# A macaron layer on one core: in the second FFN, chunk 1 takes plain products for two quarters and seven products for the other two

## The chip, the core and the metric

The kernel runs on one core of a Trainium2 chip. The metric is device time in microseconds. Three runs of the kernel before are shown, and one further execution was profiled; every time of a single instruction below comes from that profiled execution and counts from the start of its span.

## What is computed

One streaming-encoder layer on 1,024 prompt frames and 32 sample frames, 1,024 channels, all in float32. It is a half-step SwiGLU FFN, a mixer (a convolution branch and a recurrent branch), a second half-step SwiGLU FFN, and a last norm. The part that matters here is the second FFN:

```python
def _swiglu_half_step(x, g_pre, g_post, w_in, w_out):
    h = _rmsnorm(x, g_pre)
    gate, up = jnp.split(h @ w_in, 2, axis=-1)
    return x + 0.5 * _rmsnorm((jax.nn.silu(gate) * up) @ w_out, g_post)

x = x + _rmsnorm(merged @ w_out[l], g_mix_post[l])
x = _swiglu_half_step(x, g_ffn2_pre[l], g_ffn2_post[l], w_ffn2_in[l], w_ffn2_out[l])
x = _rmsnorm(x, g_final[l])
```

`w_in` has 1,024 rows and 2 x 2,816 columns. In the steps below, the norm ahead of the mixer's residual is `d`, and the norm that makes `h` for the second FFN is `e`.

## The kernel before, in words

**Layout.** Channels lie on the 128 partitions, and the 1,056 frames are cut into four quarters of 264 (`q` = 0 to 3). Quarters 0 and 1 form pair 0, quarters 2 and 3 form pair 1. The FFN's inner width is cut into 22 chunks of 128 (`i` = 0 to 21). Each float32 operand is split into a high and a low part (`split`: ScalarE copies the high part, line 93; VectorE subtracts to get the low part, line 90), and every product is three matmuls: high times high, high times low, low times high (`mm3`, lines 204 to 206).

**Two ways to make a chunk.** The plain way (`plain`, with `gemm`) makes gate (`pg`) and up (`pu`) of one quarter by 8 x 3 matmuls each, so 48 matmuls for a quarter. It needs that quarter's normed parts and the weight blocks `wh_i`, `wl_i`. The other way (`swiglu`, with `w_ops`) makes gate and up of a pair of quarters with seven products in place of eight, each over half of the channels: 7 x 4 x 3 = 84 matmuls for a pair. It needs sums of the pair's parts (`x_sums`: tiles `t`, and more `xh`, `xl`) and sums of the weights (`w_ops`: tiles `s`, `w`), both made on VectorE and ScalarE.

**The start of the second FFN.** The residual and norm chain of quarter 2 starts (`finish_w`) before the last 48 matmuls of the mixer's output product `pwo`, that of quarter 3 after them. Each chain is: three small matmuls add up squares over the partitions (`pst_d`, line 230), VectorE scales (`r_d`), GpSimd raises to the power -0.5 (`q_d`, line 234), three small matmuls spread the result over the lanes (`pst_d`, line 240), VectorE multiplies `ym` by it and adds the residual `xr_d`, ScalarE squares (`sq_e`), VectorE adds the squares (`ss_e`); then the same for norm `e` (`pst_e`, `r_e`, `q_e`, `pst_e`); then VectorE scales the channels (`f_e`, line 270) and `split` makes the parts `xh`, `xl` (`xhp`, `xlp` for the first half of the channels of an odd quarter), one half of the channels after the other.

**What sets the order.** Each engine runs its own list from the front to the end, and a scheduler makes the lists from the program's order and from priorities. The small matmuls of a chain don't stand where the chain is written: `after(n, f)` puts them off until `n` further products have been issued (12 ahead of the squares' sum of `d`, 6 ahead of the spreading, 30 ahead of the squares' sum of `e`), so they stand between other matmuls. Where the next quarter is wanted sooner than that, `drain()` issues all that was put off at once, for every quarter that waits:

```python
            if q not in h:
                drain()
            for i in range(np):
                plain(i, q)
```

Before, the second FFN makes chunks 0 and 1 in the plain way for all four quarters (`np` = 2), quarter by quarter, and then chunks 2 to 21 by seven products. The first FFN already has the form that the change gives to the second one.

Of the kernel before, what the change touches and what calls it, by code (L numbers as in the profile page):

```python
# [41 lines left out]

TAIL1, TAIL2, TAILW, OG = 4, 3, 2, 2

NP = (3, 2)

BG = (8, 3, 3, 8, 10, 9)

# [6 lines left out]
def macaron_kernel(ctx: ExitStack, tc: tile.TileContext, a: dict, o: dict):  # L55
# [27 lines left out]
    def TMP(name):  # L83
        return tp.tile([P, N], F32, tag="t", name=name)
# [4 lines left out]
    def tt(out, x, y, op):  # L89
        return nc.vector.tensor_tensor(out, x, y, op=op)  # L90
# [91 lines left out]
    def block(src, name, ahead=AHEAD, lead=0):  # L182
        with tc.high_priority(offset=ahead):
            with tc.high_priority(offset=lead):
                w = raw_block(src, name)
            h, l = (ring.tile([P, D], F32R, tag="r", name=f"w{x}_{name}") for x in "hl")
            newest_split[:] = split(h, l, w)
        return h, l
# [27 lines left out]
    def gemm(blk, h, q, name):  # L216
        b = BANK(name)[:, :N]
        while q not in h:
            later.pop(0)[1]()
        for k in range(KC):  # L220
            hi, lo = h[q][k // HC]
            mm(b, blk, k, hi[:, k % HC, :], lo[:, k % HC, :], k == 0, k == KC - 1)
        return b
# [132 lines left out]
    def x_sums(r, fe, fo, name):  # L356
        t = QUAD(F32, f"t_{name}")

        def op(k, v):
            r[k] = (QUAD(F32R, f"xh{k}_{name}"), QUAD(F32R, f"xl{k}_{name}"))  # L360
            split(*r[k], v)

        tt(t, fo[0], fe[0], OP.subtract)
        op("5", t)
        tt(t, fo[1], t, OP.subtract)
        op("6", t)
        tt(fo[0], fo[1], fo[0], OP.subtract)
        op("7", fo[0])
        tt(t, fe[1], t, OP.subtract)
        op("4", t)  # L370
# [93 lines left out]
    def ffn(x, f, h, first, mid, w_in, w_out, early, between, finish, tail, n):  # L464
# [11 lines left out]
        def in_block(i, j):  # L476
            blks.append(block(w_in[2 * i + j], f"i{n}_{i}_{j}", AHEAD if n == 2 else 0, 0 if n == 2 else 2000 if i or j else 4000))
# [5 lines left out]
        q0 = list(newest_part) if n == 1 else []  # L483
        np = NP[n - 1]
        for i in range(np):
# [6 lines left out]
        def plain(i, q):  # L492
            pg = gemm(blks[2 * i], h, q, f"pg{n}_{i}_{q}")
            pu = gemm(blks[2 * i + 1], h, q, f"pu{n}_{i}_{q}")

            def gate(pg=pg, pu=pu):
                t = TMP(f"si{n}_{i}_{q}")
                if q in held:
                    u = TMP(f"su{n}_{i}_{q}")
                    tt(t, rows[q], pg, OP.mult)  # L500
                    tt(u, rows[q], pu, OP.mult)
                    pg, pu = t, u
                nc.scalar.activation(t, pg, AF.Silu)
                tt(t, t, pu, OP.mult)
                nc.sync.dma_start(hd[i, :, q * N:(q + 1) * N], t)

            if q in held and q not in rows:
                held[q].append(gate)
            else:
                gate()  # L510

        for q in range(NQ):
# [9 lines left out]
            if c is not None:  # L522
                while builds:
                    builds.pop(0)()
                x_sums(x[c], f[2 * c], f[2 * c + 1], f"{n}_{c}")
        both = np
        if n == 1:

            both = np + 1
            for j in range(2):  # L530
                in_block(np, j)
            for q in (2, 3):
                plain(np, q)
        for i in range(np, NF):
            with behind_parts(q0 if i == np else []):
                w = w_ops(w_in[2 * i], w_in[2 * i + 1], f"{n}_{i}", WAHEAD if i < both + 2 else WLATE)
# [7 lines left out]
        for c in range(2):  # L544
# [32 lines left out]
            both = {}  # L577
# [95 lines left out]
    def finish1(q, y, ss):  # L673
# [3 lines left out]
        post1(q, y, ss, lambda: rstd(sumsq(y, f"c{q}"), f"c{q}", parts_of, CHAIN))  # L677

    finish1_last = ffn(X1, f1, {}, first1, small_constants, a["w_ffn1_in"], a["w_ffn1_out"], early1, lambda: again(0), finish1, TAIL1, 1)


# [297 lines left out]
    def finish2(q, y, ss):  # L979
# [13 lines left out]
        post_norm(y, q, ss, x2, None, f"g{q}", then)  # L993

    ffn(X2, f2, h2, lambda q, h: None, lambda: None, a["w_ffn2_in"], a["w_ffn2_out"], finish2, lambda: None, finish2, TAIL2, 2)()
    drain()

# [51 lines left out]
```

## Time and profile before

| what | value |
|---|---|
| median of three runs | 2357.35 us (2356.26 to 2358.23) |
| the profiled execution, its own time | 2356.62 us |
| its span | 2354.0 us |
| PE busy | 2323.5 us, 99% of the span, 19,148 matmuls |
| DVE (VectorE) busy | 1467.3 us, 62% |
| ACT (ScalarE) busy | 988.6 us, 42% |
| POOL (GpSimd) busy | 39.9 us, 2% |

Matmul records overlap, so a matmul's cost is the distance from its start to the next start, not its duration. Where a row ends in square brackets, the engine stood idle before it, for so long and until the named instruction was done.

### The profile page before, as it was taken

How to read it: one execution, taken by the hardware profiler on the slowest of the kernel's cores; microseconds unless marked ns; L12 is line 12 of the kernel's file. 1: busy time of each engine (PE TensorE's matmuls, PEld its weight loads, DVE VectorE, ACT ScalarE, POOL GpSimd, SP SyncE). 2: the span in 40 equal slices, each digit the busy share in tenths (PEclk: the TensorE clock that was granted, in tenths of full speed). 3: DMA queues.
4: the chain of work that ended last, by engine and by line, in shares of the span. 5: the costliest groups of instructions: out<-in, count | busy, mean ns of one | idle time of the engine just before them, and what ended most of it. 6: DMA issues, size and time to landing. Idle time of an engine off the chain costs nothing.

```text
span 2354.0 us, 44900 instructions
## 1 busy us (share of the span) xinstructions
PE 2323.5 (99%) x19148; PEld 2317.8 (98%) x19148; DVE 1467.3 (62%) x2289; ACT 988.6 (42%) x1708; POOL 39.9 (2%) x63
## 2 busy tenths in 40 slices
PE   8999999999999999999999999999999999999996
PEld 8999999999999999999999999999999999999996
DVE  6955544542657887897778966459754444542646
ACT  5533333432444554345553444244433333442432
POOL 0000000000000000000000000001000000000000
PEclk9999999999999999999999999999999999999998
DMA  5222222353655222222222554444222222353553
GB/s 177 85 82 82 78 77 74 127 192 100 237 163 179 67 92 74 83 73 83 72 76 74 184 193 166 149 133 149 80 78 77 74 82 78 123 185 106 169 175 129
DMA packets 126521, 275.17 MB, mean 117 GB/s; under 512 B 16753, under 2 KB 58737, under 8 KB 126321
## 3 DMA queue, kind: packets, MB, share of 16 engines
q1 hardware_dynamic: 126320, 272.31, 34.5%
q8 instruction: 149, 2.44, 0.4%
q14 instruction: 52, 0.42, 0.1%
HBM read 213.59 MB, written 58.67 MB: 116 GB/s over the span
## 4 chain that ended last, share of the span: by engine, by line
PE 93%; DVE 3%; DMA 1%; issue 1%; ACT 1%; POOL 0%; SPq 0%; POOLq 0%; DVEq 0%
PE p L204 11%; PE p L206 11%; PE p L205 11%; PE po L205 7%; PE po L204 7%; PE po L206 7%; PE pm L204 3%; PE pm L206 3%; PE pm L205 3%; PE pcv L204 1%; PE pco L204 1%; PE pcg L204 1%; PE pro L204 1%; PE prx L204 1%; PE prg L204 1%; PE prg L206 1%
## 5 line engine op out<-in xcount | busy, mean ns | idle before, releaser
L206 PE MATMUL p<-xh,w 128*128 128x264 f32 x2156 | 609.4, 284 | 0.2 <-DVE w L90 0.2
L205 PE MATMUL p<-xl,w 128*128 128x264 f32 x2156 | 609.4, 283 | 0.0
L204 PE MATMUL p<-xh,w 128*128 128x264 f32 x2156 | 607.1, 284 | 1.5 <-DVE prod L90 0.8
L205 PEld LDWEIGHTS p<-xl,w 128*128 128x128 f32 x2156 | 405.6, 188 | 0.0
L206 PEld LDWEIGHTS p<-xh,w 128*128 128x128 f32 x2156 | 404.9, 188 | 0.4 <-DVE w L90 0.4
L204 PEld LDWEIGHTS p<-xh,w 128*128 128x128 f32 x2156 | 402.6, 188 | 2.6 <-ACT p L93 1.3
L205 PE MATMUL po<-hl,wh_o 128*128 128x264 f32 x1408 | 397.9, 285 | 0.6 <-DVE hl L90 0.6
L206 PE MATMUL po<-hh,wl_o 128*128 128x264 f32 x1408 | 396.6, 284 | 0.0
L204 PE MATMUL po<-hh,wh_o 128*128 128x264 f32 x1408 | 392.1, 286 | 0.4 <-ACT hh L93 0.3
L205 PEld LDWEIGHTS po<-hl,wh_o 128*128 128x128 f32 x1408 | 264.8, 188 | 1.3 <-DVE hl L90 1.3
L206 PEld LDWEIGHTS po<-hh,wl_o 128*128 128x128 f32 x1408 | 264.4, 188 | 0.0
L204 PEld LDWEIGHTS po<-hh,wh_o 128*128 128x128 f32 x1408 | 260.8, 188 | 1.1 <-ACT hh L93 1.0
L90 DVE TENSOR_TENSOR wl_o<-w_o,wh_o 128x1024 fp32r<-128x1024 f32 x109 | 132.9, 1222 | 116.5 <-ACT wh_o L93 116.2
L90 DVE TENSOR_TENSOR p<-p,s 128x264 f32<-128x264 f32 x77 | 33.7, 440 | 267.3 <-ACT p L93 267.3
L721 DVE SCALAR_TENSOR_TENSOR pq<-u,vec,pq 128x542 f32<-128x542 f32 (+14 forms) x232 | 170.8, 768 | 0.0
L93 ACT ACTIVATE wh_o<-w_o 128x1024 fp32r<-128x1024 f32 x109 | 115.3, 1063 | 121.4 <-PE po L205 114.1
L90 DVE TENSOR_TENSOR w<-s,w 128x512 fp32r<-128x512 f32 x156 | 104.5, 689 | 72.6 <-ACT w L93 72.1
L93 ACT ACTIVATE p<-p 128x264 f32<-128x264 f32 x154 | 57.5, 374 | 194.4 <-PE p L206 194.4
L93 ACT ACTIVATE w<-s 128x512 fp32r<-128x512 f32 x156 | 94.1, 626 | 80.8 <-DVE s L90 78.1
L721 DVE SCALAR_TENSOR_TENSOR rs<-rs,wsum 128x542 f32<-128x542 f32 (+6 forms) x112 | 86.0, 768 | 0.0
L90 DVE TENSOR_TENSOR s<-s,s 128x264 f32<-128x264 f32 x56 | 23.9, 429 | 98.7 <-ACT s L315 98.5
L90 DVE TENSOR_TENSOR hl<-hf,hh 128x1056 fp32r<-128x1056 f32 x44 | 55.2, 1254 | 46.4 <-ACT hh L93 46.2
(465 smaller groups left out, 5720.2 us busy)
## 6 DMA issues: line engine op xcount, KB each, us to landing
w_o<-in_w_ffn_out SPq DMA_DIRECT2D x109, 512.0 KB, 3.8
hf<-hd SPq DMA_DIRECT2D x44, 528.0 KB, 5.2
hd<-prod SPq DMA_DIRECT2D x77, 264.0 KB, 2.1
w_g<-in_w_ffn_in SPq DMA_DIRECT2D x39, 512.0 KB, 3.7
w_u<-in_w_ffn_in SPq DMA_DIRECT2D x39, 512.0 KB, 3.7
w_wo<-in_w_out SPq DMA_DIRECT2D x18, 512.0 KB, 3.7
sgd<-sg SPq DMA_DIRECT2D x32, 264.0 KB, 2.1
gs<-sgd SPq DMA_DIRECT2D x16, 528.0 KB, 6.7
```

What stands on the lines that cost most here:

```text
L90: return nc.vector.tensor_tensor(out, x, y, op=op)
L93: return nc.scalar.activation(out, x, AF.Copy)
L204: nc.tensor.matmul(out, wh, xh, start=first, stop=False, skip_group_check=True)
L205: nc.tensor.matmul(out, wh, xl, start=False, stop=False, skip_group_check=True)
L206: newest_mm[:] = [nc.tensor.matmul(out, wl, xh, start=False, stop=last, skip_group_check=True).ins]
L721: nc.vector.scalar_tensor_tensor(acc[c][:, d:], src[c][:, :HW - d], wt[c](d), acc[c][:, d:], op0=OP.mult, op1=OP.add)
```

## The change

The first number of `NP` is for the first FFN, the second for the second one. The second FFN now makes only chunk 0 in the plain way for all four quarters. Chunk 1 gets the plain way for quarters 2 and 3 and the seven products for pair 0; its weights are read twice, once as blocks and once for `w_ops`. Chunk 2 keeps its two separate passes by pair, and from chunk 3 on nothing changes.

```diff
-NP = (3, 2)
+NP = (3, 1)
...
-        both = np
-        if n == 1:
-
-            both = np + 1
-            for j in range(2):
-                in_block(np, j)
-            for q in (2, 3):
-                plain(np, q)
+
+        both = np + 1
+        for j in range(2):
+            in_block(np, j)
+        for q in (2, 3):
+            plain(np, q)
         for i in range(np, NF):
             with behind_parts(q0 if i == np else []):
                 w = w_ops(w_in[2 * i], w_in[2 * i + 1], f"{n}_{i}", WAHEAD if i < both + 2 else WLATE)
             for cs in ((0,),) if i < both else ((0,), (1,)) if i == both else ((0, 1),):
                 end = hidden(i, w, cs)
```

Two places of the engines' lists follow. In them `pg_0_2` is the gate of chunk 0, quarter 2, and the number behind it only tells tiles apart; `xh_2_2`, `xl_2_2` are parts of quarter 2, and `xhp_3`, `xlp_3` of quarter 3.

TensorE before, where the small matmuls of norm `e` stand; first those of quarter 2, within the gate of chunk 0, quarter 1:

```order
L204 MATMUL pg_0_1_18711<-xhp_1_18306,wh_i_0_0_18509 128x264
L205 MATMUL pg_0_1_18711<-xlp_1_18307,wh_i_0_0_18509 128x264
L206 MATMUL pg_0_1_18711<-xhp_1_18306,wl_i_0_0_18510 128x264
L230 MATMUL pst_e_18715<-ones,ss_e_18571 88x1 x3
L204 MATMUL pg_0_1_18711<-xhp_1_18306,wh_i_0_0_18509 128x264
```

Behind this sum stand 18 matmuls of the same gate, then the spreading of quarter 2 (line 240), then 30 more matmuls. TensorE before, 50 rows further on, the sum of quarter 3 within the gate of chunk 1, quarter 1:

```order
L204 MATMUL pg_1_1_18794<-xhp_1_18306,wh_i_1_0_18521 128x264
L205 MATMUL pg_1_1_18794<-xlp_1_18307,wh_i_1_0_18521 128x264
L206 MATMUL pg_1_1_18794<-xhp_1_18306,wl_i_1_0_18522 128x264
L230 MATMUL pst_e_18798<-ones,ss_e_18665 88x1 x3
L204 MATMUL pg_1_1_18794<-xhp_1_18306,wh_i_1_0_18521 128x264
```

Here too 18 matmuls stand ahead of the spreading, and behind it 27 more ahead of the first product of quarter 2.

TensorE now, at the end of the up product of chunk 0, quarter 1, where `drain()` has issued both chains:

```order
L206 MATMUL pu_0_1_18670<-xh_2_1_18315,wl_i_0_1_18516 128x264
L230 MATMUL pst_e_18699<-ones,ss_e_18559 88x1 x3
L240 MATMUL pst_e_18699<-ident,q_e_18705 128x88 x3
L230 MATMUL pst_e_18707<-ones,ss_e_18653 88x1 x3
L240 MATMUL pst_e_18707<-ident,q_e_18713 128x88 x3
L204 MATMUL pg_0_2_18757<-xh_2_2_18723,wh_i_0_0_18509 128x264
L204 MATMUL pu_0_2_18782<-xh_2_2_18723,wh_i_0_1_18515 128x264
L205 MATMUL pg_0_2_18757<-xl_2_2_18724,wh_i_0_0_18509 128x264
L206 MATMUL pg_0_2_18757<-xh_2_2_18723,wl_i_0_0_18510 128x264
```

The 93 matmuls that stood between the first sum and the first product of quarter 2 are gone from there: the four groups stand side by side, and behind them at once quarter 2's first product.

VectorE before, from the low part of quarter 2's first half to that of quarter 3's first half:

```order
L90 TENSOR_TENSOR xl_2_2_18750<-f_e_0_18744,xh_2_2_18749 128x4x264
L270 SCALAR_TENSOR_TENSOR f_e_1_18753<-ym_1_17328,vec,pst_e_18715 128x264 x4
L90 TENSOR_TENSOR s_2_19148<-w_u_2_19137 128x512
L90 TENSOR_TENSOR s_2_2_19157<-w_g_2_19135,w_u_2_19137 128x512
L90 TENSOR_TENSOR xl_2_2_18759<-f_e_1_18753,xh_2_2_18758 128x4x264
L270 SCALAR_TENSOR_TENSOR f_e_0_18827<-ym_0_17329,vec,pst_e_18798 128x264 x4
L90 TENSOR_TENSOR si_1_1_18873<-si_1_1_18873,pu_1_1_18848 128x264
L90 TENSOR_TENSOR w_2_2_19150<-s_2_19148,w_2_2_19150 128x512
L90 TENSOR_TENSOR s_2_19148<-s_2_19148,w_g_2_19135 128x512
L90 TENSOR_TENSOR xlp_3_18833<-f_e_0_18827,xhp_3_18832 128x4x264
```

VectorE now, the same stretch:

```order
L90 TENSOR_TENSOR xl_2_2_18724<-f_e_0_18718,xh_2_2_18723 128x4x264
L270 SCALAR_TENSOR_TENSOR f_e_1_18727<-ym_1_17328,vec,pst_e_18699 128x264 x4
L90 TENSOR_TENSOR w_2_1_19042<-s_1_19040,w_2_1_19042 128x512
L90 TENSOR_TENSOR s_2_1_19049<-w_g_1_19027,w_u_1_19029 128x512
L90 TENSOR_TENSOR xl_2_2_18733<-f_e_1_18727,xh_2_2_18732 128x4x264
L270 SCALAR_TENSOR_TENSOR f_e_0_18739<-ym_0_17329,vec,pst_e_18707 128x264 x4
L90 TENSOR_TENSOR s_1_19040<-s_1_19040,w_g_1_19027 128x512
L90 TENSOR_TENSOR si_0_2_18807<-si_0_2_18807,pu_0_2_18782 128x264
L90 TENSOR_TENSOR xlp_3_18745<-f_e_0_18739,xhp_3_18744 128x4x264
```

The weight sums between the parts are now those of chunk 1. The product of gate and up that stands ahead of `xlp_3` was that of quarter 1, and is now that of quarter 2, whose matmuls need `xl_2_2` of a few rows above.

## Rows read from the trace of the kernel before

**Rows 1.** The page's head, and its table of busy time by engine.

```profile
span 2354.0 us, 44900 instructions
PE 2323.5 (99%) x19148; PEld 2317.8 (98%) x19148; DVE 1467.3 (62%) x2289; ACT 988.6 (42%) x1708; POOL 39.9 (2%) x63
```

**Rows 2.** The timeline of PE: start, duration, instruction, idle time before it.

```profile
1620.52 0.44 PE L240 MATMUL pst_d<-ident,q_d 88*128 88x88 f32 x3 [0.33 <-POOL q_d L234]
...
1625.32 0.56 PE L230 MATMUL pst_e<-ones,ss_e 128*88 128x1 f32 x6
...
1628.14 0.44 PE L240 MATMUL pst_e<-ident,q_e 88*128 88x88 f32 x3
...
1632.10 0.56 PE L230 MATMUL pst_e<-ones,ss_e 128*88 128x1 f32 x6
...
1645.60 0.29 PE L204 MATMUL pg<-xh,wh_i 128*128 128x264 f32 x1
...
1647.05 0.28 PE L204 MATMUL pu<-xh,wh_i 128*128 128x264 f32 x1
```

**Rows 3.** Busy time by stretch of 20 us: length, each engine's busy time and instructions.

```profile
1620.00:1640.00 20.00, 19.67 (x167) 19.31 (x166) 18.24 (x33) 6.31 (x10) 3.05 (x3) 1.00 0.50 161
...
1660.00:1680.00 20.00, 20.00 (x165) 19.80 (x164) 16.99 (x23) 9.08 (x17) 0.00 (x0) 1.00 0.19 59
```

**Rows 4.** The timeline of DVE, quarters 2 and 3 of the second FFN.

```profile
1621.00 1.25 DVE L90 TENSOR_TENSOR ym<-ym,pst_d 128x1056 f32<-128x1056 f32 x1 [1.24 <-PE pst_d L240]
...
1623.95 0.42 DVE L90 TENSOR_TENSOR ss_e<-sq_e 128x264 f32<-128x264 f32 x1
...
1625.25 1.32 DVE L90 TENSOR_TENSOR ym<-ym,xr_d 128x528 f32<-128x528 f32 x2
1626.49 0.15 DVE L232 TENSOR_SCALAR r_e<-pst_e 88x3 f32<-88x3 f32 x1
...
1628.62 0.49 DVE L270 SCALAR_TENSOR_TENSOR f_e<-ym,vec,pst_e 128x264 f32<-128x264 f32 x1
...
1630.04 0.43 DVE L90 TENSOR_TENSOR ss_e<-sq_e 128x264 f32<-128x264 f32 x1
...
1632.77 0.16 DVE L232 TENSOR_SCALAR r_e<-pst_e 88x3 f32<-88x3 f32 x1 [0.33 <-PE pst_e L230]
...
1633.44 0.68 DVE L90 TENSOR_TENSOR w<-w_u,w 128x512 fp32r<-128x512 f32 x1
1634.04 1.25 DVE L90 TENSOR_TENSOR xl<-f_e,xh 128x1056 fp32r<-128x1056 f32 x1
1635.21 1.68 DVE L270 SCALAR_TENSOR_TENSOR f_e<-ym,vec,pst_e 128x264 f32<-128x264 f32 x4
1636.82 0.68 DVE L90 TENSOR_TENSOR s<-w_u 128x512 f32<-128x512 f32 x1
```

**Rows 5.** The timeline of POOL and of ACT in the same stretch.

```profile
1619.09 1.37 POOL L234 TENSOR_TENSOR q_d<-r_d,mhalf 88x3 f32<-88x3 f32 x1 [6.38 <-DVE r_d L232]
1626.72 1.36 POOL L234 TENSOR_TENSOR q_e<-r_e,mhalf 88x3 f32<-88x3 f32 x1 [6.26 <-DVE r_e L232]
...
1625.99 1.26 ACT L260 ACTIVATE sq_e<-ym 128x528 f32<-128x528 f32 x2 [0.25 <-DVE ym L90]
...
1631.64 1.08 ACT L93 ACTIVATE xh<-f_e 128x1056 fp32r<-128x1056 f32 x1 [2.23 <-DVE f_e L270]
```

**Rows 6.** PE alone by microsecond at the tail: length, busy, granted clock.

```profile
2332.00:2333.00 1.00, 1.00 (x9) 1.00 1.03 354
...
2335.00:2336.00 1.00, 0.02 (x1) 0.62 0.00 0
2336.00:2337.00 1.00, 0.68 (x3) 0.50 0.00 0
```

**Rows 7.** The timeline of PE at launch, two of the 21 matmuls in a row.

```profile
9.86 0.42 PE L204 MATMUL pg<-gh,wh_i 128*128 128x264 f32 x1
...
14.23 0.28 PE L206 MATMUL pg<-gh,wl_i 128*128 128x264 f32 x1
```

## The prediction

> **What bounds the kernel now.** I read the page first: PE is busy for 2323.5 of 2354.0 us, in 19,148 matmuls, and no engine but it for more than 62% of the span [rows 1]. So the time moves in two ways alone: by the number of matmuls, and by holes in PE's list. The change works in one place, the start of the second FFN, so I read the timelines there, engine by engine. PE is dense. Twelve matmuls start within 1645.60 to 1647.05, which is 0.121 us each [rows 2]. The only hole is small: it waits 0.33 us for `q_d` of quarter 3 [rows 2]. But what feeds PE there is nearly as full: VectorE is busy for 18.24 of 20 us from 1620 on, and still 16.99 from 1660 on [rows 3]. It works through the chains of quarters 2 and 3, and PE's plain products of quarters 0 and 1 are the cover under which it does so. The change takes half of that cover away.
>
> **What the change removes and adds.** Chunk 1 of pair 0 took 2 x 48 plain matmuls and now takes 84: 12 fewer at 0.121 us, **-1.45 us**. That is all that it gives. It adds the reading and the sums of chunk 1's weights a second time: 1 MB more to load, seven splits and four sums on VectorE at 0.60 us each [rows 4], about 6.6 us, of which two gates' work at 0.35 us goes away. Its two loads stand where those of chunk 2 stood, and those of chunk 2 one place later, some 40 us ahead of their products: hidden under all the plain ones; a load that came late would cost PE just its delay.
>
> **What it moves.** Before, some 93 ordinary matmuls, 11 us, stood between the squares' sum of quarter 2's norm `e` and the first product of quarter 2. Now none do: `drain()` has put the sums and the spreadings of both quarters side by side, ahead of that product. PE runs its list in order, as the 0.33 us row shows: the matmul behind the spreading had all it needed and still waited for `q_d`. So PE stands until quarter 3's chain has come that far, though its next product needs only quarter 2. When is that? I walk both lists with the distances between starts in the rows.
>
> PE: the spreading of `d` for quarter 3 can't move up. It waits for `q_d`, whose 1.37 us begin at 1619.09 [rows 5], so it starts at 1620.52 as before. But four matmuls that stood ahead of it now stand behind: **+0.5 us**. PE goes on at 1620.96 with 38 matmuls, less the one that goes out during the spreading, and comes to the drained groups at about 1625.45.
>
> VectorE: the first `ym` multiply starts at 1621.00 as before [rows 4]. Then stand `ss_e` of quarter 2 (0.42 long, 0.35 to the next start, as a step starts 0.08 before the last one's end in these rows), the second multiply (1.17), one gate (0.35) and four residual adds (0.62 each, two from 1625.25 to 1626.49 [rows 4]), to about 1626.6. The first add of squares (0.62) follows; its squares, 0.63 us each on ACT [rows 5], are done by then. `r_e` of quarter 2 starts at 1627.25, where it started at 1626.49 before. From `r_e` to GpSimd it is 0.23 us, from there to the spreading 1.42 (1626.72 to 1628.14), from that to `f_e` 0.48 [rows 2, 4, 5]. So the spreading of quarter 2 is at 1628.9, and `f_e` at 1629.4. VectorE's list has that `f_e` ahead of the last square adds of quarter 3, so these wait too: `f_e` 0.40, add 0.62, `f_e` 0.40, `ss_e` 0.42, end at 1631.2. It ended at 1630.47 before [rows 4]. Quarter 3 then needs 0.67 from the sum to `r_e` (1632.10 to 1632.77 [rows 2, 4]), 0.23 and 1.42 again: its spreading is at 1633.5. Two products need the high part alone and slip in. The third needs `xl_2_2`: the fourth `f_e` ends at 1632.5, `xh` takes 1.08 on ACT [rows 5], VectorE does two weight steps (0.60 each) meanwhile, `xl` takes 1.17 [rows 4]. So PE is dense again at 1634.9.
>
> That hole is 9.45 us, from 1625.45. The four small groups (0.44 each [rows 2]) and two products run in it and ran before too, so it costs 9.45 - 1.76 - 0.24, **+7.45 us**.
>
> **The clock.** PE's last dense matmul of the whole run ends in the 2333rd microsecond. The granted clock falls in the stretch from 2335 to 2336, and stands at 0.50 (the lower level, 1.2 of 2.4 GHz) behind it, with a few small matmuls between [rows 6]. The hole here is three times as long and just as empty, so I expect the lower level when PE comes back. At launch the first matmuls start 0.22 us apart: 20 of them from 9.86 to 14.23, then 0.12 [rows 7]. The products of quarter 2's first half are 22: at 0.22 instead of 0.121 they cost **+2.15 us**. A warm PE would lose 1.0 of these anyway, waiting for the second half's `xl`: four `f_e` (1.61), two weight steps and the split (1.17) are 4.0 us behind the first half's, so 1638.9, and 22 warm matmuls would be over at 1637.6. So the clock itself costs 1.15 here. The Trainium skill's page "TensorE: Matmul & The Clock Gate", section "HAM oscillation — how this bites in real kernels", has the same fall behind long gaps, and counts the penalty as half of the throttled time, which for 22 x 0.22 = 4.8 us is an estimate of 2.4 us. By that the sum below would be 1.2 us higher; no row can say yet, and I keep the walk.
>
> Behind that the second half's 24 matmuls run from 1639.7 to 1642.65. VectorE's list now has quarter 2's gate product (`si_0_2`) ahead of `xlp_3`, and it needs the last of these matmuls, so `xlp_3` is done at 1644.5. The list of PE has 11 matmuls of chunk 1 for just that time; only `xhp_3` is late, by **+0.3 us**. From 1647.45 PE has all it needs.
>
> **What is late next.** The sums for chunk 1 (pair 0) and chunk 2 stand on a VectorE that is full and carries about 6 us more. On the same walk chunk 1's products begin at 1660.4 and find their parts. Those of chunk 2 don't: the fifth product's weights are ready at 1673.2 on ACT while PE comes to them at 1672.1 (1.1), the sixth's low part is 0.4 late, a bank copied by ACT behind weight splits 0.4, and a bank to be read first 0.15: **+2.05 us**. Bounds: nothing, if VectorE's steps are a little shorter, and 5 us, if none of the 6 us added finds a gap. From chunk 3 on VectorE has slack again.
>
> **Sum.** -1.45 + 0.5 + 7.45 + 2.15 + 0.3 + 2.05 = **+11.0 us**. The profiled execution took 2356.62 us, 2.62 over its span, so 2367.6; the median of the runs lies 0.73 above it, at 2357.35, so 2368.4. I say **2368 us**, 0.45% slower. About 0.2%, 4.7 us, can be told from no change.
>
> **Rivals.**
> *The hole is shallower.* The clock recovers at once or never falls (-1.15), and VectorE's later work fits (-2.05): +7.8 us, so 2364 to 2366. For it: the lower level came only 2.5 us after the last dense matmul at the tail, and some small groups lie in our hole. Against: only four such groups in over 9 us.
> *The clock stays low.* Where PE is fed in bursts, it may remain at 0.50 until 1647. Then the second half takes 5.3 us, the 11 + 24 products behind it 7.7, and PE has all it needs 5.7 us later than above: 2374; with VectorE's full 5 us, 2377. For it: PE gets quarter 2 and 3 half by half from a chain that needs 4 us for each. Against: at launch the first 21 matmuls were enough, and PE is never empty for more than 0.5 us from 1634.9 on.
> *Not slower.* The groups drained together find their sums done, because without the products of chunk 1 between them VectorE's chain of quarter 3 is over when PE arrives at 1625.45. Then only -1.45 and the later waits are left, 2356 to 2358. It decides at `ss_e` of quarter 3: to be covered it must end by then. For it: that chain holds 1.24 us in which VectorE waits for PE's spreading. Against: it ends at 1630.47 before, 5 us too late, and the wait is for GpSimd's `q_d`, which nothing here makes earlier. A chain 3 us shorter would still leave some 5 us of hole.
>
> **How the numbers follow.** The forecast 0.62, the shallower hole 0.13, the low clock 0.16, not slower 0.09. The range holds the forecast with its bounds, the shallower hole, and most of the low clock: 2363 to 2376. The first three are slower by over 0.2%, 0.90 with a little taken off for a shallower hole that stays under 4.7 us; of the rest nearly all is within 0.2%: 0.08, and faster 0.02.
>
> **What would show it.** In the timeline of PE after 1625: four small groups with the waits named (`q_e`, then `ss_e`, then `q_e` again), next to nothing else until about 1635, granted clock 0.50 there, and matmul starts 0.22 us apart behind it. In the table of waits of PE: some 7 us by `ss_e`, `q_e` and `xl` together. Between 1665 and 1680 short waits for ACT's or VectorE's `w`. It would be wrong if PE's small groups of quarter 3 don't hold up quarter 2, or if the list's order is not what the chip runs.

## The result, and the profile after

The changed kernel takes 2367.14 us (median of five, 2366.81 to 2374.41) against 2356.59 us (five, 2356.01 to 2358.23): a ratio of 1.0054, interval 1.0043 to 1.0064, so 0.54% slower. In a second set it took 2368.03 against 2355.75, ratio 1.0058 (1.0046 to 1.0071). Both agree with the forecast of 2368, but the place where the time goes is dearer than the forecast's sum, as its rows show.

The head of the page and the table of busy time, which answer to [rows 1]:

```profile
span 2365.3 us, 44911 instructions
PE 2326.9 (98%) x19136; PEld 2319.9 (98%) x19136; DVE 1475.6 (62%) x2302; ACT 993.6 (42%) x1718; POOL 39.6 (2%) x63
```

Twelve matmuls fewer, as the change says, and thirteen VectorE instructions more: seven splits, four sums and four steps of the seven products, in place of two gates. The timeline of PE at the start of the second FFN, which answers to [rows 2]:

```profile
1618.75 0.44 PE L240 MATMUL pst_d<-ident,q_d 88*128 88x88 f32 x3 [0.66 <-POOL q_d L234]
...
1623.67 0.56 PE L230 MATMUL pst_e<-ones,ss_e 128*88 128x1 f32 x6
1627.20 0.70 PE L240 MATMUL pst_e<-ident,q_e 88*128 88x88 f32 x3 [2.97 <-POOL q_e L234]
1629.93 1.01 PE L230 MATMUL pst_e<-ones,ss_e 128*88 128x1 f32 x6 [2.04 <-DVE ss_e L90]
1632.19 0.70 PE L240 MATMUL pst_e<-ident,q_e 88*128 88x88 f32 x3 [1.25 <-POOL q_e L234]
1632.77 0.59 PE L204 MATMUL pg<-xh,wh_i 128*128 128x264 f32 x1
...
1634.07 0.59 PE L205 MATMUL pg<-xl,wh_i 128*128 128x264 f32 x1 [0.48 <-DVE xl L90]
...
1640.17 0.33 PE L205 MATMUL pg<-xl,wh_i 128*128 128x264 f32 x1
...
1642.40 0.28 PE L206 MATMUL pu<-xh,wl_i 128*128 128x264 f32 x1
1642.81 0.39 PE L204 MATMUL pg<-xhp,wh_i 128*128 128x264 f32 x1
```

From 1623.67 to 1634.07 PE does four small groups and two products, and waits by name for `q_e`, `ss_e`, `q_e` and `xl`. Before, the same groups had no wait at all [rows 2]. From 1634.07 to 1640.17 there are 28 matmuls, 0.218 us each; behind 1640.17 they stand 0.12 apart, until the first product with `xhp` comes 0.41 behind its predecessor. The granted clock in PE's view by microsecond (length, busy, clock, DMA share, GB/s) says why they are slow:

```profile
1626.00:1627.00 1.00, 0.00 (x0) 0.81 1.02 363
1627.00:1628.00 1.00, 0.70 (x3) 0.50 0.60 208
...
1639.00:1640.00 1.00, 1.00 (x7) 0.50 0.45 180
1640.00:1641.00 1.00, 1.00 (x9) 0.87 0.00 0
```

The clock fell to the lower level while PE waited for the first `q_e`, and rose again behind the 28 matmuls. By the rows at its two ends (0.81 and 0.87) it was low for 13.6 us. The timeline of DVE, which answers to [rows 4]:

```profile
1625.54 0.15 DVE L232 TENSOR_SCALAR r_e<-pst_e 88x3 f32<-88x3 f32 x1
...
1629.36 0.43 DVE L90 TENSOR_TENSOR ss_e<-sq_e 128x264 f32<-128x264 f32 x1
...
1631.05 0.16 DVE L232 TENSOR_SCALAR r_e<-pst_e 88x3 f32<-88x3 f32 x1 [0.52 <-PE pst_e L230]
1631.13 0.47 DVE L270 SCALAR_TENSOR_TENSOR f_e<-ym,vec,pst_e 128x264 f32<-128x264 f32 x1
...
1642.79 0.43 DVE L90 TENSOR_TENSOR si<-si,pu 128x264 f32<-128x264 f32 x1 [2.57 <-ACT xhp L93]
1643.14 1.25 DVE L90 TENSOR_TENSOR xlp<-f_e,xhp 128x1056 fp32r<-128x1056 f32 x1
```

Here the two chains are put into each other: `r_e` and the last `f_e` of quarter 2 stand around the sum of quarter 3, and the `r_e` of quarter 3 has to come in ahead of that last `f_e`. Two rows of ACT name what VectorE's wait of 2.57 us for `xhp`, and PE's short one, hang on:

```profile
1641.39 0.39 ACT L503 ACTIVATE si<-pg 128x264 f32<-128x264 f32 x1 [4.65 <-PE pg L206]
1641.68 1.08 ACT L93 ACTIVATE xhp<-f_e 128x1056 fp32r<-128x1056 f32 x1
```

The copy of quarter 3's high part stands behind quarter 2's gate on ScalarE, and that gate waited 4.65 us for PE's slow matmuls. Last, the waits of PE from 1600 to 1700, those at the last of chunk 1's seven products (`prod`) and at the products of chunk 2 (total, times, longest):

```profile
PE p L204 <- ACT w L93: 0.9, 1, 0.9
...
PE p L204 <- DVE prod L90: 0.3, 1, 0.3
PE p L206 <- DVE w L90: 0.2, 1, 0.2
PE p L204 <- ACT p L93: 0.2, 1, 0.2
```

Each costs somewhat more than it shows. By the starts, these four matmuls stand 0.59, 1.15, 0.50 and 0.49 us behind their predecessors, and the next one behind each 0.23: 3.6 us for eight steps, where 8 x 0.121 is 1.0. So the four waits cost 2.7 us.

### The profile page after: what moved, and what is told of

It is laid out like the page before. It is cut to its first block, busy times and chain, and to the rows that moved or that the text cites. A ratio compares the mean times of both kernels' runs of the same rounds, so it can differ in the third digit from the quotient of the medians.

```text
span 2365.3 us, 44911 instructions
## 1 busy us (share of the span) xinstructions
PE 2326.9 (98%) x19136; PEld 2319.9 (98%) x19136; DVE 1475.6 (62%) x2302; ACT 993.6 (42%) x1718; POOL 39.6 (2%) x63
## 4 chain that ended last, share of the span: by engine, by line
PE 92%; DVE 4%; issue 1%; DMA 1%; ACT 1%; POOL 0%; SPq 0%; POOLq 0%; DVEq 0%; ACTq 0%
PE p L204 11%; PE p L206 11%; PE p L205 11%; PE po L205 7%; PE po L204 7%; PE po L206 7%; PE pm L204 3%; PE pm L206 3%; PE pm L205 3%; PE pcv L204 1%; PE pco L204 1%; PE pcg L204 1%; PE pro L204 1%; PE prx L204 1%; PE prg L204 1%; PE prg L206 1%
## 5 line engine op out<-in xcount | busy, mean ns | idle before, releaser
L204 PE MATMUL p<-xh,w 128*128 128x264 f32 x2184 | 615.5, 285 | 2.9 <-DVE prod L90 1.2
L206 PE MATMUL p<-xh,w 128*128 128x264 f32 x2184 | 617.5, 284 | 0.4 <-DVE w L90 0.4
L205 PE MATMUL p<-xl,w 128*128 128x264 f32 x2184 | 617.3, 283 | 0.0
L204 PEld LDWEIGHTS p<-xh,w 128*128 128x128 f32 x2184 | 408.0, 188 | 4.4 <-DVE prod L90 1.6
L205 PEld LDWEIGHTS p<-xl,w 128*128 128x128 f32 x2184 | 411.0, 188 | 0.0
L206 PEld LDWEIGHTS p<-xh,w 128*128 128x128 f32 x2184 | 410.1, 188 | 0.8 <-DVE w L90 0.8
```

Of the source, the lines that this page charges most:

```text
L204: nc.tensor.matmul(out, wh, xh, start=first, stop=False, skip_group_check=True)
L205: nc.tensor.matmul(out, wh, xl, start=False, stop=False, skip_group_check=True)
L206: newest_mm[:] = [nc.tensor.matmul(out, wl, xh, start=False, stop=last, skip_group_check=True).ins]
```

## The experiments

Each kernel was timed against the kernel before on the same chip. Since executions of one kernel differ by some 4 us, the profiles are also compared by a distance that leaves most of this out: from the spreading of norm `d` of quarter 3 (line 240, the last row ahead of the change) to the first product with `w_out` (`po`, line 204), some 450 us later. The first row is shown above for both kernels (1620.52 [rows 2] and 1618.75); the second one is this, in the kernel before and then in the changed one:

```profile
2069.20 0.29 PE L204 MATMUL po<-hh,wh_o 128*128 128x264 f32 x1
```

```profile
2080.95 0.29 PE L204 MATMUL po<-hh,wh_o 128*128 128x264 f32 x1
```

The first mark lies anywhere from 1618.75 to 1621.51 in profiles with the same number of matmuls ahead of it, and the changed kernel's repetition has it at 1619.50, so the 1.77 us of lead in the changed kernel's profile are not counted as the change's. Between the marks the changed kernel has 8 matmuls fewer than the one before, and not 12: the four that stood ahead of the first mark now stand behind it.

| kernel | median us (before) | ratio, interval | marks | distance | over before |
|---|---|---|---|---|---|
| before | | | 1620.52, 2069.20 | 448.68 | |
| changed | 2367.14 (2356.59) | 1.0054, 1.0043 to 1.0064 | 1618.75, 2080.95 | 462.20 | +13.5 |
| e0_again | 2368.03 (2355.75) | 1.0058, 1.0046 to 1.0071 | 1619.50, 2082.33 | 462.83 | +14.2 |
| e8_order | 2364.39 (2355.49) | 1.0039, 1.0025 to 1.0053 | 1620.28, 2077.93 | 457.65 | +9.0 |
| e2_cover | 2357.31 (2355.49) | 1.0013, 1.0004 to 1.0022 | 1621.19, 2070.87 | 449.68 | +1.0 |
| e9_half | 2359.75 (2355.91) | 1.0017, 1.0008 to 1.0026 | 1619.26, 2073.53 | 454.27 | +5.6 |
| e1_own | 2370.77 (2355.75) | 1.0065, 1.0052 to 1.0078 | 1620.63, 2084.61 | 463.98 | +15.3 |
| e10_noadd | 2366.34 (2355.91) | 1.0043, 1.0029 to 1.0057 | 1620.11, 2080.55 | 460.44 | +11.8 |
| e4_fill | 2367.32 (2355.75) | 1.0052, 1.0040 to 1.0065 | 1619.73, 2080.19 | 460.46 | +11.8 |
| e5_pool | 2373.31 (2355.75) | 1.0075, 1.0061 to 1.0089 | 1622.04, 2083.62 | 461.58 | +12.9 |
| e6_seven | 2374.82 (2355.49) | 1.0083, 1.0069 to 1.0097 | 1619.82, 2088.77 | 468.95 | +20.3 |
| e3_only7 | 2372.39 (2355.49) | 1.0073, 1.0060 to 1.0085 | 1621.51, 2085.40 | 463.89 | +15.2 |

**e0_again: the changed kernel, unedited,** as the measure for the others.

> The changed kernel once more, beside the next three on the same chip: 10 to 11 us over the kernel before, about 2367 us. In its first profile the quarter-3 spreading of norm d ran at 1618.75, where the kernel before had it at 1620.52. If that lead belongs to the one execution, it comes out otherwise here while the time stays; if the change causes it, it is there again.

It repeats the result within 1 us. Its first product with `xl` starts here:

```profile
1635.50 0.59 PE L205 MATMUL pg<-xl,wh_i 128*128 128x264 f32 x1 [0.48 <-DVE xl L90]
```

That is 16.0 us behind its mark, where the changed kernel's first profile has 15.3. Two executions of one kernel thus differ by 0.7 us in the hole, and the steps below are compared with both.

**e8_order: the lost cover alone,** with all matmuls and weights of the kernel before (the diff is against that one).

```diff
-            for i in range(np):
+            for i in range(np if n == 1 or q > 1 else 1):
                 plain(i, q)
...
+        if n == 2:
+            for q in (0, 1):
+                plain(1, q)
```

> The kernel before with the same matmuls, weights and sums, but with chunk 1's plain products of quarters 0 and 1 (96 matmuls) moved from ahead of quarter 2 to behind quarter 3. Nothing is read or summed twice. Theory A: the same hole as in the changed kernel, some 8 to 9 us behind the first squares' sum of norm e, the granted clock at 0.50 behind it and matmuls 0.22 us apart; no gain of 1.45 and no later waits of 2.3: 2356.6 + 11.5 or so, 2366 to 2369. Rival B (the mixed form's weights and sums): no more than 2 us from the kernel before, 2355 to 2359.

It is 9 us slower than before, by the medians and by the marks, half a microsecond under theory A's 9.4 to 12.4. PE's timeline has the hole of the changed kernel:

```profile
1624.76 0.56 PE L230 MATMUL pst_e<-ones,ss_e 128*88 128x1 f32 x6
1627.89 0.70 PE L240 MATMUL pst_e<-ident,q_e 88*128 88x88 f32 x3 [2.58 <-POOL q_e L234]
1630.63 1.01 PE L230 MATMUL pst_e<-ones,ss_e 128*88 128x1 f32 x6 [2.03 <-DVE ss_e L90]
...
1634.76 0.59 PE L205 MATMUL pg<-xl,wh_i 128*128 128x264 f32 x1
```

```profile
1637.00:1638.00 1.00, 1.00 (x10) 0.92 0.00 0
```

The granted clock is at 0.50 from 1627 until it rises in this microsecond, so it is low for 10.2 us. From the first sum to the first product with `xl` it is 10.0 us, against 10.4 in the changed kernel. Nothing is read or summed twice here, so rival B (no more than 2 us) falls.

**e2_cover: the mixed form with the cover left in place.** Chunk 1 stays plain, and chunk 2 takes the form of the change.

```diff
-NP = (3, 1)
+NP = (3, 2)
```

> Same form, one chunk later: chunks 0 and 1 are plain for all four quarters, as in the kernel before, and it is chunk 2 that takes plain products for quarters 2 and 3 and seven products for pair 0. So the weights of a chunk are still read and summed twice, but the 93 matmuls stand again ahead of quarter 2. Theory A (the lost cover is the cost): no hole by q_e and ss_e at 1625, and only 12 matmuls more than before, +1.45 us, and at most some 2 us of waits for weights: 2357 to 2360. Rival B (the mixed form itself, its second reading and its sums on a full VectorE, is the cost): 2362 or more, with waits of PE for w or s behind 1660.

It is 1.8 us slower than before by the medians and 1.0 by the marks, for 12 matmuls more (1.45), of which 8 stand between the marks (0.97). Three of its eleven runs lie at 2362 to 2364, for a cause that no profile shows; with them the interval of the ratio still ends at 1.0022, 5.2 us, short of rival B's 2362. PE's waits from 1600 to 1700 are two, and neither is for weights or sums:

```profile
PE pst_d L240 <- POOL q_d L234: 0.6, 1, 0.6
PE pst_e L240 <- POOL q_e L234: 0.5, 1, 0.5
```

VectorE is as full there as in the changed kernel, which has it busy for 19.84 us of the same stretch (windows of 20 us, as in [rows 3]):

```profile
1660.00:1680.00 20.00, 20.00 (x168) 20.00 (x167) 19.95 (x26) 10.47 (x17) 0.00 (x0) 1.00 0.28 83
```

It is busy for 19.95 of 20 us, and PE has no wait there. The double weights are hidden where there is PE work ahead of them.

**e9_half: half of the cover.** Only chunk 1's products of quarter 1 are moved (against the kernel before).

```diff
-            for i in range(np):
+            for i in range(1 if n == 2 and q == 1 else np):
                 plain(i, q)
...
+        if n == 2:
+            plain(1, 1)
```

> Half of the cover: the kernel before, with chunk 1's plain products of quarter 1 alone (48 matmuls, 5.8 us) moved from ahead of quarter 2 to behind quarter 3; those of quarter 0 stay ahead. If the cost is the time by which the chain of quarter 2 outlasts PE's cover, each matmul taken away costs its 0.121 us from the point where the cover is used up: PE comes to quarter 2 some 5.8 us later than with both moved, 1 us ahead of xh and 3 to 3.5 us ahead of the first xl, with no pause of over 2.5 us, so the clock stays up: 3 to 4 us over the kernel before, about a third of what moving both cost (8.9). If the cost comes at once with any such move, or with the clock: 6 us or more. If half the cover is enough: within 1 us of the kernel before.

By the medians it costs 3.8 us, as expected, by the marks 5.6, near the 6 that a cost with the clock was to give. The second wait was smaller than expected (1.31 us, and not 3 to 3.5), and the clock fell all the same, which was not expected. PE's timeline, and its view by microsecond:

```profile
1631.51 0.39 PE L204 MATMUL pg<-xh,wh_i 128*128 128x264 f32 x1 [0.89 <-ACT xh L93]
...
1633.58 0.47 PE L205 MATMUL pg<-xl,wh_i 128*128 128x264 f32 x1 [1.31 <-DVE xl L90]
```

```profile
1633.00:1634.00 1.00, 0.42 (x2) 0.87 0.00 0
1634.00:1635.00 1.00, 1.00 (x9) 0.50 0.00 0
...
1640.00:1641.00 1.00, 1.00 (x8) 0.71 0.00 0
```

Two short waits make 2.2 us. Behind them 28 matmuls stand about 0.22 us apart until 1640.67, some 2.8 us more for the clock. So the expected cost came about in another way, half of it through the clock.

**e1_own: quarter 2 doesn't stand behind quarter 3's groups.** The sum and spreading of quarter 3 go between quarter 2's products.

```diff
-            if q not in h:
+            if q not in h and n == 2:
+                later.pop(0)[1]()
+                later.pop()[1]()
+                later[:] = [(terms[0] + 4, e[1]) for e in later]
+            elif q not in h:
                 drain()
```

> The changed kernel, but ahead of quarter 2 only quarter 2's own chain is issued; quarter 3's small matmuls stand between quarter 2's products again. Theory A (the prediction's words: PE stands until quarter 3's chain has come that far): the hole of 9.5 us ends when quarter 2's spreading is there, some 3 to 4 us sooner, so 2363 to 2364 us. Theory B (quarter 2's own parts are the last thing waited for, and VectorE makes them no sooner, since ss_e of quarter 3 stands between its steps either way): f_e of quarter 2 no longer waits for r_e of quarter 3, xl comes 0.8 us sooner, and the time falls by 1 us or less, 2366 to 2367 us.

It is slower than the changed kernel, by 2.7 us in the same set, which neither theory had. PE's timeline:

```profile
1634.37 0.59 PE L204 MATMUL pg<-xh,wh_i 128*128 128x264 f32 x1 [4.20 <-ACT xh L93]
...
1635.66 0.59 PE L205 MATMUL pg<-xl,wh_i 128*128 128x264 f32 x1 [0.49 <-DVE xl L90]
...
1643.54 0.39 PE L240 MATMUL pst_e<-ident,q_e 88*128 88x88 f32 x3
```

The wait for quarter 3 has gone, and one of 4.20 us for quarter 2's own `xh` has taken its place. The first product with `xl` comes 15.03 us behind the mark, in the changed kernel's two profiles 15.32 and 16.00: 0.3 to 1.0 us is all that quarter 3's groups held up, about the 0.8 of theory B. Quarter 3's spreading, now behind matmuls at the low clock, comes 22.9 us behind the mark in place of 13.4, so quarter 3 is later. That its delay is what makes this kernel slower isn't shown apart.

**e10_noadd: 2.5 us less on VectorE,** in the middle of both chains. It leaves out the four residual adds of quarter 3, so that quarter's output lacks the residual; only its time is of use.

```diff
-                    tt(y[h][:, j:j + 2, :], y[h][:, j:j + 2, :], xr, OP.add)
+                    if name != "d3":
+                        tt(y[h][:, j:j + 2, :], y[h][:, j:j + 2, :], xr, OP.add)
```

> The changed kernel without the four residual adds of quarter 3 ahead of the second FFN (the output of quarter 3 lacks the residual there; its data are still loaded): VectorE has 2.5 us less to do in the middle of the hole, and TensorE's list is nearly the same (the sum of quarter 3 stands two products later). Theory A (the hole is as long as VectorE needs for both chains, put one into the other): r_e of quarter 2 comes about 1.2 us sooner and the first product with xl 2 to 3 us sooner, 2 to 3.5 us less than the changed kernel, 2364 to 2366. Rival B (what PE waits for is the round trip of sum, power and spreading, which no add lengthens): within 1 us of the changed kernel's 2367 to 2368.

Two rows of PE:

```profile
1631.41 0.59 PE L204 MATMUL pg<-xh,wh_i 128*128 128x264 f32 x1 [4.13 <-ACT xh L93]
...
1633.03 0.59 PE L205 MATMUL pg<-xl,wh_i 128*128 128x264 f32 x1
```

The product with `xl` comes 12.92 us behind the mark, 2.4 to 3.1 sooner, as theory A had it. Between the marks 1.8 to 2.4 us are saved, by the medians 0.8 to 1.7 against other sets. The median is 0.3 us beyond the expected 2364 to 2366, and the interval of its ratio overlaps that of the changed kernel, so it is the marks and the rows that bear A out here.

**e4_fill: PE kept at work in the hole.** It adds 38 products of quarter 1's data whose sums nobody reads, 20 ahead of quarter 2's spreading and 18 behind it (`name` is the norm and the quarter).

```diff
+    def fill_hole(count):
...
+        with behind():
+            for _ in range(count):
+                newest_mm[:] = [nc.tensor.matmul(b, filler[1], hi, start=True, stop=True, skip_group_check=True).ins]
...
+            fill_hole(20 if name == "e2" else 8)
...
+            if name == "e2":
+                fill_hole(10)
```

> The changed kernel with 38 more matmuls in the hole, on data of quarter 1, into a PSUM bank that nothing reads: 20 ahead of quarter 2's spreading and 18 behind it. Nothing of the computation changes. If the low clock behind the hole costs what the rows say (28 matmuls 0.22 us apart, and small matmuls that take 1.0 in place of 0.56 us, less what VectorE holds back anyway), the granted clock stays at 1.00 and the time falls by 1.5 to 2.5 us, to about 2365 us. If VectorE alone sets the pace there, the clock stays up and the time stays at 2367 us within 0.5. If the added matmuls delay the chain, it is slower than 2367 us.

Between the marks it saves 1.7 us against the changed kernel's profile and 2.4 against its second one; by the medians 0.7 in the same set, less than the expected 1.5 to 2.5. PE's view by microsecond shows that the clock still fell, but later and for less long:

```profile
1634.00:1635.00 1.00, 0.96 (x7) 0.76 0.00 0
...
1637.00:1638.00 1.00, 1.00 (x7) 0.53 0.00 0
```

It is low for 3.4 us in place of 13.6. The hole itself is nearly as long (first `xl` product 14.92 us behind the mark, 0.4 to 1.1 sooner): the clock is the smaller part of the loss, the wait the larger.

**e5_pool: seven weight splits of chunk 1 moved from VectorE to GpSimd.**

```diff
-                split(r[k][:, 0, :], r[k][:, 1, :], v)
+                split(r[k][:, 0, :], r[k][:, 1, :], v, nc.gpsimd if name == "2_1" else None)
```

> The changed kernel with the low parts of chunk 1's seven weight splits made on GpSimd in place of VectorE, which gives VectorE back 7 x 0.60 = 4.2 us. Theory A (the hole is a chain of waits, not VectorE's load): the hole stays; only the short waits of 1665 to 1680 shrink, by some 1.1 of 2.3 us, so 2366 us. Theory C (the loss is VectorE's added load): the time falls by about 4 us, to 2363 us. If GpSimd's own steps hold up q_d or q_e, it is slower, 2369 us or more.

It is slower. The timelines of POOL and of PE show the splits ahead of the norm of quarter 2:

```profile
1608.96 3.43 POOL L97 TENSOR_TENSOR w<-w_g,w 128x512 fp32r<-128x512 f32 x2 [15.47 <-ACT w L93]
1612.35 1.26 POOL L97 TENSOR_TENSOR w<-w_u,w 128x512 fp32r<-128x512 f32 x1
1613.57 0.84 POOL L234 TENSOR_TENSOR q_d<-r_d,mhalf 88x3 f32<-88x3 f32 x1
```

```profile
1614.47 0.44 PE L240 MATMUL pst_d<-ident,q_d 88*128 88x88 f32 x3 [3.29 <-POOL q_d L234]
```

PE waits 3.29 us for `q_d`, ahead of the mark, and the chain is later by that; so this run doesn't tell what a freer VectorE is worth.

**e6_seven: the seven products of pair 0 as the cover,** ahead of quarter 2.

```diff
+            if n == 2 and q == 2:
+                x_sums(x[0], f[0], f[1], f"{n}_0")
+                hidden(np, w_ops(w_in[2 * np], w_in[2 * np + 1], f"{n}_{np}", WAHEAD), (0,))
```

> The changed kernel with the seven products of chunk 1 for pair 0 (84 matmuls, 10.2 us) moved from behind quarter 3 to ahead of quarter 2, so that PE has cover again and 12 matmuls fewer than before. But pair 0's sums and chunk 1's weight sums are then wanted in the 20 us in which VectorE is busy for 18. If any work of PE at that place is enough: 2355 to 2357, no worse than before. If VectorE is the limit: PE waits there for t, s or w in place of q_e, the chains of quarters 2 and 3 are put off by the sums, and the time is 2360 to 2370; this is what I expect.

It is the slowest of all, 4.8 us beyond the expected range. PE's waits from 1600 to 1700 name the sums and weights of that cover:

```profile
PE p L204 <- ACT w L93: 4.1, 2, 3.1
PE pg L205 <- DVE xl L90: 2.6, 2, 1.9
PE p L206 <- DVE w L90: 1.6, 2, 0.9
```

Cover that needs VectorE first is none: the chain of quarter 2 is late behind it, and PE waits for both.

**e3_only7: without chunk 1's plain products for quarters 2 and 3,** twelve matmuls fewer again.

```diff
-        both = np + 1
...
-        for q in (2, 3):
-            plain(np, q)
+        both = np
+        if n == 1:
...
```

> The changed kernel without chunk 1's plain products for quarters 2 and 3: seven products for pair 0 and, apart, for pair 1. Twelve matmuls fewer again (-1.45), no second reading of chunk 1's weights as blocks. But these 96 matmuls filled PE from 1640 to 1660, while VectorE made the sums. If the count of matmuls decides: 2365 to 2366. If VectorE's sums are what is late there: PE waits for t, w or s between 1645 and 1665, several us in all, 2368 to 2374.

It is slower than the changed kernel, in the range that the theory of late sums gave. Between the marks it costs 1.1 to 1.7 us more than the changed kernel, less than the 4 to 5 by the medians. The longest of PE's waits for a sum's part, of two for `xh` and two for `xl` that come to 3.6 us, is this row:

```profile
1658.02 0.39 PE L204 MATMUL p<-xh,w 128*128 128x264 f32 x1 [1.45 <-ACT xh L93]
```

## Why the prediction was right, and where it was not

**The mechanism was right.** e8_order has the lost cover without the double weights and costs 9 us; e2_cover has the double weights without the lost cover and costs 1.0 to 1.8 us, about its 12 matmuls. Of the changed kernel's 13.5 us between the marks some 4.5 are left. By its rows 2.7 are the later waits, about 1.6 a clock that is low for 13.6 us in place of e8_order's 10.2, about 1 a longer hole and the wait for `xhp`, less 1.0 for 8 matmuls fewer. The rival in which the sums are done when PE arrives is refuted by PE's waits; that in which the clock stays low until 1647 by the row of 1640; the shallower hole by the 28 slow matmuls and the later waits.

**The walk against the rows,** in us behind the mark:

| step | walk | changed |
|---|---|---|
| PE at the drained groups | 4.93 | 4.92 |
| spreading, quarter 2 | 8.4 | 8.45 |
| end of `ss_e`, quarter 3 | 10.7 | 11.04 |
| spreading, quarter 3 | 13.0 | 13.44 |
| first product with `xl` | 14.4 | 15.32 |
| end of `xlp_3` | 24.0 | 25.64 |
| PE has all it needs | 26.9 | 28.71 |

**The hole** was 0.9 us too small in the walk (1.6 by e0_again), for the most part since it took the small groups at the duration that they have at the full clock. At the lower level the spreading lasts 0.70 in place of 0.44 and the squares' sum 1.01 in place of 0.56; VectorE stood idle 0.52 us for it, then did quarter 3's `r_e` and only then the last `f_e` of quarter 2.

**The clock** was mis-sized: 28 matmuls at 0.22 and not 22, so 2.7 us in place of 2.15. The walk gave the clock itself 1.15, since a warm PE would wait 1.0 of its 2.15 anyway. Counted so, it is 1.7 behind the hole, and with the 0.7 by which the two longer groups hold up the chain, which the walk left out, an estimate of 2.4. e4_fill, which takes away three quarters of the low stretch, saves 1.7 to 2.4 between the marks, but 0.7 by the medians, so the size is not settled. The Trainium skill's page "TensorE: Matmul & The Clock Gate", section "HAM oscillation — how this bites in real kernels", counts half of the throttled time as the penalty. The prediction's estimate of 2.4 by it comes to the same, but for another stretch: half of all the 13.6 us in which the clock was low would be an estimate of 6.8 by that page of the Trainium skill, and more than half of those 13.6 us is the hole itself, where PE mostly waits.

**`xhp_3`** was right: 0.3 forecast, and PE's first product with it comes 0.41 behind its predecessor in place of 0.12. What it hangs on is ScalarE's list, where the copy stands behind quarter 2's gate. PE has all it needs 1.8 us later than in the walk, of which 0.9 is the hole's, 0.6 the six more slow matmuls, and the rest slower first starts behind waits.

**The later waits** were right in kind and somewhat small: 2.7 us, 2.05 forecast, the longest for the weights named. The bank to be read first (`prod`) cost 0.47 in place of 0.15, and the matmul behind each wait 0.1 more. The prediction counted the added splits and sums, but not the four VectorE steps of the seven products, of which `prod` is one. **The 12 matmuls** are there too. So 10.4 + 1.8 + 2.7 - 1.45 is 13.45 (the 10.4 are the walk's terms up to there), against 13.5 between the marks and 11.0 forecast.

**Why the total fitted nonetheless.** That execution came to the place 1.77 us earlier than the one before, and took 284.35 us from the second mark to the end where that one took 284.80: 13.52 - 1.77 - 0.45 is the 11.3 between the spans. The medians, 10.6 and 12.3 us apart, are lower than the marks too. Why the kernel as a whole gives back 1 to 3 us of what is lost between the marks is not settled; the profiles are one execution each. So the mechanism was no luck; that the total came out within 1 us of 2368 was, in part: the terms were 2.5 us too small together, and the rest of the execution hid that.

**The clause that failed** is that PE stands until quarter 3's chain has come that far, though its next product needs only quarter 2. e1_own took quarter 3's groups out of the way, and the product came 0.3 to 1.0 us sooner, in a kernel that was slower as a whole. PE's list named quarter 3, but VectorE works through both chains as one, and quarter 2's own parts were just as late; e10_noadd, which shortens that list by 2.5 us, brought 2.4 to 3.1. The prediction's time didn't hang on the clause, since the walk went through VectorE's list.

## What to carry to other kernels

Matmuls that look dear may be the cover of a serial chain: before saving 12 of them, count what stands between the chain's first step and the first product that needs its last, and how much longer the chain is than what is left. Cover is good only if it is ready: plain products of data that has long been there cost a few matmuls, products that need sums first made it worse. Where a wait names one chain, take that one out before believing it: another of the same length on the same engine may stand behind it.

## What the runs showed of the hardware

The granted clock fell in e9_half behind waits of 0.89 and 1.31 us with four matmuls between them, and stayed at 0.50 until 1640, though PE worked without a pause from 1634 on. In e2_cover, with waits of 0.6 and 0.5 us at this place, and in before, where the longest is 0.33 us [rows 2], it stays at 1.00 [rows 3].

GpSimd took 1.3 to 2.3 us for a split of 128x512 in e5_pool that takes VectorE 0.68 [rows 4]; the profiler's spans on GpSimd are rough.

The changed kernel has a second place without slack. In the profiled execution of e0_again PE waited at the output product for a part copied by ScalarE, and the granted clock fell to 0.50 there too, in the microsecond from 2109:

```profile
2107.61 0.88 PE L204 MATMUL po<-hh,wh_o 128*128 128x264 f32 x5 [1.77 <-ACT hh L93]
```

That execution took 2372.88 us where the set's median is 2368.03, and 288.77 us from the second mark to the end in place of 284.35. The profile of e3_only7, 2375.75 us where its median is 2372.39, has the same: a wait of 2.21 us for `hh`, the clock at 0.50 behind it, and 288.60 us to the end. In all other profiles, where the clock doesn't fall there, it is 284.2 to 286.0. Whether the other high runs have this cause is not shown.
